# Hybrid decoder trunk: another order of the experts behind the first pair, and routing by token halves

## The chip, the cores and the metric

One Trainium2 chip, one of its cores. The time is device microseconds (us) of one execution of the whole program, taken as the median of several runs. The program has no collective and one launch.

## The reference, cut to what matters

Two layers over 256 tokens of 1024 channels, all in 32-bit floats. Each layer is a mixer (windowed attention beside a gated linear recurrence), a LayerNorm, a feed-forward part and a second LayerNorm. The feed-forward part of layer 0 is one dense SwiGLU. That of layer 1 is a mixture of eight experts with 3584 hidden channels each, and every token goes to its two best experts:

```python
logits = jnp.einsum('bsd,de->bse', x, router_w).astype(f32)
top_val, top_idx = lax.top_k(logits, TOP_K)
top_p = jax.nn.softmax(top_val, axis=-1)
comb = jnp.sum(top_p[..., None] * jax.nn.one_hot(top_idx, N_EXPERTS, dtype=f32), axis=-2)
y = jnp.zeros(x.shape, f32)
for e in range(N_EXPERTS):
    y = y + comb[..., e:e + 1] * _swiglu(x, w_gate[e], w_up[e], w_down[e]).astype(f32)
```

The 256 tokens make 512 assignments to eight experts, some 64 per expert. The weights of all eight experts are read.

## The kernel before, in words

**The stream of weights.** All weights come in units of 1 MB (`WeightStream`, L46), in the order in which they are multiplied, on the one DMA queue of SyncE (SP). A unit is loaded (L104) when a slot of on-chip memory for it is free. There are five slots from the start; in layer 1 scratch memory is added bit by bit, the last of it at L1008 to L1015 (two of the split buffers, four slots `wx0` to `wx3` under the scratch of the mixer, and `ax`), so that the experts begin with 15 slots (14 once `ax` is taken back in block 0 of place 1). A unit that needs an expert's number (every unit of experts other than expert 0) has SP load the number from `idi` first.

**Wide and narrow experts.** The experts are worked through in eight places 0 to 7. Place 0 is always expert 0. The others are ranked by their token counts, and `SEQ[s]` (L39) is the rank that place `s` takes, `CAP[s]` (L40) the tokens it has room for. With 128 it is wide: each weight unit is split into a high and a low half (`_hi` on ScalarE, L125, `_lo` on VectorE, L143), and TensorE multiplies three times in `fp32r` (hi by hi, lo by hi, hi by lo). The slot is free after `_lo`, some units ahead of TensorE. With 64 it is narrow: the unit is multiplied as it is, in two halves of the array's columns, and the slot is free after TensorE.

An expert has seven blocks of 512 hidden channels with six units each (two gate, two up, two down), 42 units in all. Places 0 and 1 are interleaved block by block (`blocks`, L264); this is called the pair. Places 2 to 7 follow one after the other. The loop at L1226 does gate, Silu, up, the product, and then the down projection of the block before. `start_expert` (L1093) gathers an expert's tokens by multiplying them with a one-hot matrix, `finish_expert` (L1171) adds its output to the residual.

**The stretch before the experts (L985 to L1201).** The order on each engine is the order in which this Python emits it. The two halves of 128 tokens, t = 0 and 1, come out of the mixer's output projection one after the other. For each, VectorE subtracts the mean (`center`), TensorE transposes the result for the router, and `normalise` multiplies on VectorE (L959) and adds on GpSimd (POOL, L961). `logits` are 16 small matmuls, `select` (L974) finds each token's top two on VectorE in six small instructions. The positions of the tokens within each expert come from one set of matmuls for both halves (L1035), `expert_one_hot(0)` makes the one-hot matrix, `route_ranks` (L1178) ranks the experts by count in 16 small instructions on VectorE and writes their numbers to `idi`, and `start_expert(0)` gathers. Matmuls without use (`keep_warm`, L421) fill waits of TensorE. In the first block `route_experts` (L1203) works out the weights of the tokens and the capacities on VectorE.

Of the kernel before, what the change touches and what calls it, by code (L numbers as in the profile page):

```python
# [16 lines left out]
P = 128  # L17
# [7 lines left out]
E = 8  # L25
# [13 lines left out]
SEQ = (None, 3, 0, 4, 1, 5, 2, 6)  # L39
CAP = (128, 64, 128, 64, 128, 64, 64, 64)  # L40
# [5 lines left out]
class WeightStream:  # L46
    def __init__(self, tc, pool, units):
        self.nc = tc.nc
        self.units = units
        self.loaded = 0  # L50
        self.n_hi = 0
        self.n_lo = 0
        self.taken = 0
        self.w = {}
        self.hl = {}
        self.owner = {}
        self.free = [(pool, f"w{j}") for j in range(NW_BASE)]
        self.ring = {p: [(pool, f"{p}{j}") for j in range(NHI)] for p in ("hi", "lo")}
        self.first = None
        self.after = {}  # L60
        self.lent = None

# [20 lines left out]
    def _fill(self):  # L83
        while self.free and self.loaded < len(self.units):
            self._load()

# [112 lines left out]
def trunk(ctx, tc, x, xT, w_in, w_out, prm, wbd, rb, ohc, cst, ln1_g, ln1_b, ln2_g, ln2_b,  # L199
# [115 lines left out]
    U = WeightStream(tc, wpool, units)  # L315

# [7 lines left out]
    jmask = csts[:, 256:384].rearrange("p (t a b) -> p t a b", t=2, a=8)  # L324
# [649 lines left out]
    def select(t, p):  # L974
        V.scalar_tensor_tensor(lg[:, t, :], p[:, 0:E], ln[t].mv[:, 1:2], rwb, op0=ALU.mult, op1=ALU.add)
        le = lg[:, t, :, None].to_broadcast([P, E, E])
        lj = lg[:, t, None, :].to_broadcast([P, E, E])
        c = cmp[:, t]
        V.tensor_tensor(out=c[:, :, 0, :], in0=lj, in1=le, op=ALU.is_equal)
        V.tensor_tensor(out=c[:, :, 0, :], in0=c[:, :, 0, :], in1=jmask[:, t], op=ALU.mult)  # L980
        V.tensor_tensor(out=c[:, :, 1, :], in0=lj, in1=le, op=ALU.is_gt)
        V.tensor_reduce(out=rank[:, t, :], in_=c.rearrange("p e a j -> p e (a j)"), op=ALU.add, axis=AX.X)
        V.tensor_scalar(sel[:, t, :], rank[:, t, :], 1.5, None, op0=ALU.is_lt)

# [15 lines left out]
    keep_warm(1, big())  # L1000
    for q in range(2):
        transpose_x(ax[:, 1, :], q, xf_emit(1))
    keep_warm(2, big())
    normalise(1)
    select(0, plg)
    select(1, logits(1))
    keep_warm(7, big())
# [10 lines left out]
    pos = rt.tile([P, 2, E], F32, name="pos")  # L1018
# [8 lines left out]
    cmp7 = ep.tile([P, E - 1, 2, E - 1], F32, name="cmp7")  # L1027
# [6 lines left out]
    pp = sm()  # L1034
    mm(pp[:, 0:2 * E], trir, sel.rearrange("p t e -> p (t e)"), True, False)  # L1035
    mm(pp[:, E:2 * E], onesr, sel[:, 0, :], False, True)
    pc = sm()
    for t in range(2):
        mm(pc[:, 0:E], onesr, sel[:, t, :], t == 0, t == 1)
    keep_warm(3, halves()[0])  # L1040
    V.tensor_copy(pos, pp[:, 0:2 * E].rearrange("p (t e) -> p t e", t=2))
# [51 lines left out]
    def start_expert(s):  # L1093
        wide = CAP[s] == P
        g = [ep.tile([P, KC, CAP[s]], F32R if wide else F32, name=f"g{s}_{i}", tag="g", bufs=3)
             for i in range(1 + wide)]

        def dst(a, p):
            A.activation(g[0][:, a, :], p, AF.Copy)
            if wide:  # L1100
                V.tensor_tensor(out=g[1][:, a, :], in0=p, in1=g[0][:, a, :].bitcast(F32), op=ALU.subtract)  # L1101

        gather(ohe[s], dst, CAP[s])
        st[s] = g
# [73 lines left out]
    def route_ranks():  # L1178
        V.tensor_copy(cnt8, pc[:, 0:E])
        n = E - 1  # L1180
        le = cnt8[:, 1:E, None].to_broadcast([P, n, n])
        lj = cnt8[:, None, 1:E].to_broadcast([P, n, n])
        V.tensor_tensor(out=cmp7[:, :, 0, :], in0=lj, in1=le, op=ALU.is_equal)
        V.tensor_tensor(out=cmp7[:, :, 0, :], in0=cmp7[:, :, 0, :], in1=jmask[:, 0, 1:E, 1:E], op=ALU.mult)
        V.tensor_tensor(out=cmp7[:, :, 1, :], in0=lj, in1=le, op=ALU.is_gt)
        V.tensor_reduce(out=rank7, in_=cmp7.rearrange("p e a j -> p e (a j)"), op=ALU.add, axis=AX.X)
        for s in range(1, E):
            V.tensor_scalar(perm[:, s - 1, :], rank7, float(SEQ[s]), None, op0=ALU.is_equal)
        V.tensor_scalar(id7, iota[:, 1:E], UNSEL, None, op0=ALU.add)
        V.tensor_tensor(out=tmp7, in0=perm, in1=id7[:, None, :].to_broadcast([P, n, n]), op=ALU.mult)  # L1190
        V.tensor_reduce(out=id7, in_=tmp7, op=ALU.add, axis=AX.X)
        V.tensor_copy(idi, id7[0:1, :])

    expert_one_hot(0)
    V.tensor_reduce(out=mxl, in_=lg, op=ALU.max, axis=AX.X, negate=True)
    route_ranks()
# [4 lines left out]
    start_expert(0)  # L1201

    def route_experts():  # L1203
        n = E - 1
        V.tensor_tensor(out=pr, in0=pr, in1=selv, op=ALU.mult)
# [20 lines left out]
    for i, (s, b) in enumerate(blocks):  # L1226
# [6 lines left out]
        if i == 0:  # L1233
            route_experts()
        if (s, b) == (1, 0):
            assert U.lent is None
            ax = mxp.tile([P, 2, D], F32, name="axm", tag="ax")
            for t in range(2):
                scaled(t)
# [119 lines left out]
def _layout(i):  # L1359
# [67 lines left out]
    cst[:, 256:384] = np.tile((np.arange(8)[None] < np.arange(8)[:, None]).reshape(1, 64), 2)  # L1427
# [21 lines left out]
```

## Time and profile before

| what | value |
|---|---|
| time, median of 3 runs | 1282.12 us (1280.95 to 1283.67) |
| the profiled execution, its own time | 1284.04 us |
| its span, first to last instruction | 1282.3 us |
| TensorE busy with matmuls | 1224.8 us, 96% |
| VectorE busy | 647.4 us, 50% |
| ScalarE busy | 518.1 us, 40% |
| moved by DMA | 428.99 MB, 335 GB/s over the span |

The span is what the trace shows from the first to the last instruction; the time of the execution has 1.7 us more around it. A busy TensorE is not one at its peak: a matmul counts as busy while it is in the pipe. The DMA rate by slices of the span says more here, since the experts' weights come at one rate for long stretches.

### The profile page before, as it was taken

Reading aid. Unit: us, or ns where it says so; the run is one execution under the profiler, and the core shown is the slowest. Engines: PE = TensorE matmul, PEld = TensorE weight load, DVE = VectorE, ACT = ScalarE, POOL = GpSimd, SP = SyncE. Lnnn points to the kernel's source line nnn. Section 1 sums busy time; section 2 is a strip of 40 time slices with the busy share of each in tenths; the row PEclk is TensorE's granted clock in tenths of the full one; section 3 lists DMA queues with packets and bytes.
Section 4 is the critical chain, followed back from the end, with each engine's and each line's share of the span. In section 5 each row is a group of like instructions: output and inputs, shape, how many; then the busy total and the mean of one; then the engine's idle time right before and its main releaser. Section 6 shows DMA issues by size and latency. Waiting matters only on the chain. (4 is left out here: it accounts for less than half of the span.)

```text
span 1282.3 us, 18541 instructions
## 1 busy us (share of the span) xinstructions
PE 1224.8 (96%) x7564; PEld 911.7 (71%) x7564; DVE 647.4 (50%) x616; ACT 518.1 (40%) x549; POOL 81.0 (6%) x75
## 2 busy tenths in 40 slices
PE   9999999999999899999999999999999999799884
PEld 8979999999987776666678875568886554354441
DVE  6597544457688753445588841069882001001004
ACT  5674443344683542444467731057762000000001
POOL 3124000004022010000000000000000000000001
PEclk9999999999999999999999999999999999999998
DMA  9843545554377769999999979999999999999994
GB/s 350 310 176 143 208 176 196 198 213 150 149 285 276 272 249 415 420 421 420 421 420 414 367 278 420 420 420 421 421 421 392 420 420 421 420 420 420 421 420 180
DMA packets 63506, 428.99 MB, mean 335 GB/s; under 512 B 7951, under 2 KB 8376, under 8 KB 12984
## 3 DMA queue, kind: packets, MB, share of 16 engines
q1 hardware_dynamic: 62408, 423.55, 81.8%
q0 software_dynamic: 720, 3.68, 0.8%
q8 instruction: 61, 1.00, 0.3%
q10 hardware_dynamic: 288, 0.52, 0.1%
q14 instruction: 29, 0.24, 0.0%
HBM read 426.67 MB, written 2.63 MB: 335 GB/s over the span
## 5 line engine op out<-in xcount | busy, mean ns | idle before, releaser
L143 DVE TENSOR_TENSOR lo<-w,hi 128x2048 fp32r<-128x2048 f32 (+1 forms) x181 | 402.6, 2242 | 88.5 <-ACT hi L125 87.4
L125 ACT ACTIVATE hi<-w 128x2048 fp32r<-128x2048 f32 (+1 forms) x183 | 340.6, 1875 | 92.3 <-PE sm L240 52.8
L240 PE MATMUL sm<-w,g 128*64 128x256 f32 x2240 | 265.8, 382 | 4.3 <-DMA w<-in_moe_w_up_dram 4.2
L240 PEld LDWEIGHTS sm<-w,g 128*64 128x64 f32 x2240 | 159.2, 137 | 100.2 <-issue 23.7
L240 PE MATMUL sm<-hi,g 128*128 128x512 f32 x672 | 220.8, 400 | 1.5 <-DVE g L1101 1.5
L1242 DVE TENSOR_TENSOR h<-h,sm 128x256 f32<-128x256 f32 (+1 forms) x56 | 29.0, 518 | 294.7 <-PE sm L240 290.3
L240 PE MATMUL acc<-w,ht 128*64 128x512 f32 x560 | 141.5, 603 | 20.3 <-DMA w<-in_moe_w_down_dram 19.7
L1140 ACT ACTIVATE ht<-sm 128x256 f32<-128x256 f32 (+1 forms) x56 | 25.6, 457 | 322.4 <-PE sm L1138 322.4
L240 PEld LDWEIGHTS sm<-hi,g 128*128 128x128 f32 x672 | 126.7, 189 | 33.4 <-DVE g L1101 2.0
L240 PE MATMUL sm<-lo,g 128*128 128x512 f32 x336 | 133.7, 398 | 3.3 <-DVE lo L143 3.3
L240 PE MATMUL sm<-xh,hi 128*128 128x256 f32 x528 | 132.5, 284 | 0.0
L240 PE MATMUL sm<-xl,hi 128*128 128x256 f32 x528 | 132.0, 283 | 0.0
L240 PEld LDWEIGHTS acc<-w,ht 128*64 128x64 f32 x560 | 40.8, 138 | 99.2 <-issue 70.3
L240 PE MATMUL acc<-hi,ht 128*128 128x512 f32 x336 | 109.8, 398 | 0.0
L240 PEld LDWEIGHTS sm<-xh,hi 128*128 128x128 f32 x528 | 99.6, 189 | 1.7 <-issue 1.3
L240 PEld LDWEIGHTS sm<-xl,hi 128*128 128x128 f32 x528 | 99.8, 189 | 0.4
L240 PE MATMUL sm<-xh,lo 128*128 128x256 f32 x528 | 84.8, 283 | 0.0
L240 PEld LDWEIGHTS sm<-lo,g 128*128 128x128 f32 x336 | 63.5, 189 | 18.4 <-DVE lo L143 4.3
L240 PEld LDWEIGHTS acc<-hi,ht 128*128 128x128 f32 x336 | 63.0, 187 | 17.3 <-issue 2.7
L240 PEld LDWEIGHTS sm<-xh,lo 128*128 128x128 f32 x528 | 72.3, 189 | 0.0
L240 PE MATMUL acc<-lo,ht 128*128 128x512 f32 x168 | 67.1, 400 | 5.1 <-DVE lo L143 5.1
L353 POOL TENSOR_TENSOR mv<-mv,mhalf 128x1 f32<-128x1 f32 x8 | 7.0, 877 | 815.4 <-DVE mv L352 815.4
(263 smaller groups left out, 1177.7 us busy)
## 6 DMA issues: line engine op xcount, KB each, us to landing
w<-in_moe_w_gate_dram SPq DMA_DIRECT2D x112, 1024.0 KB, 13.7
w<-in_moe_w_up_dram SPq DMA_DIRECT2D x112, 1024.0 KB, 14.3
w<-in_moe_w_down_dram SPq DMA_DIRECT2D x110, 1024.0 KB, 15.7
w<-in_w_in_dram SPq DMA_DIRECT2D x18, 1024.0 KB, 6.1
w<-in_ffn_w_gate_dram SPq DMA_DIRECT2D x11, 1024.0 KB, 4.8
w<-in_ffn_w_up_dram SPq DMA_DIRECT2D x11, 1024.0 KB, 5.7
w<-in_ffn_w_down_dram SPq DMA_DIRECT2D x11, 1024.0 KB, 6.1
w<-in_w_out_dram SPq DMA_DIRECT2D x8, 1024.0 KB, 4.8
```

Source lines behind the costliest of these rows:

```text
L125: self.nc.scalar.activation(hi[a], w[a], AF.Copy)
L143: V.tensor_tensor(out=lo[a], in0=w[a], in1=hi[a].bitcast(F32), op=ALU.subtract)
L240: T.matmul(o, l, r, start=first, stop=last)
L353: G.tensor_tensor(out=o, in0=o, in1=mhalf, op=ALU.pow)
L1140: A.activation(ht[0], p[:, 0:nj, :], AF.Copy)
L1242: V.tensor_tensor(out=h, in0=h, in1=pu, op=ALU.mult)
```

## The change

It has four parts. (1) `SEQ` and `CAP` change: behind the pair the places are narrow, wide, narrow, wide, narrow, narrow, in place of wide, narrow, wide, narrow, narrow, narrow. The ranks that get 128 and 64 places stay the same. (2) The router's work is done for each half of the tokens by itself: half 0 is selected before half 1 is normalised, and expert 0's gather is done in two parts (`first_gather`), for half 0 while half 1 is still being selected, accumulating in two banks that are held meanwhile. Its one-hot matrix `oh0` lies in slot 8 of the mixer's scratch; the one in the place of before is made in the first block instead, for `finish_expert` alone. Ten of the 13 matmuls without use go. (3) `route_ranks` compares one key per expert (eight times the count, less the expert's number) in place of counts with a rule for ties, and takes 7 instructions in place of 16; it stands behind the gather's evictions. (4) Loads stop at a limit, before the first unit that needs an expert's number, until `route_ranks` has been emitted (`open`).

```diff
-SEQ = (None, 3, 0, 4, 1, 5, 2, 6)
-CAP = (128, 64, 128, 64, 128, 64, 64, 64)
+SEQ = (None, 3, 4, 0, 5, 1, 2, 6)
+CAP = (128, 64, 64, 128, 64, 128, 64, 64)
...
     def _fill(self):
-        while self.free and self.loaded < len(self.units):
+        while self.free and self.loaded < self.limit:
             self._load()
+
+    def open(self):
+        self.limit = len(self.units)
+        self._fill()
...
+    U.limit = len(units) - len(blocks) * 6 + [s for s, _ in blocks].index(1) * 6 - 2
...
-    jmask = csts[:, 256:384].rearrange("p (t a b) -> p t a b", t=2, a=8)
+    jmask = csts[:, 256:320].rearrange("p (a b) -> p a b", a=8)
+    seqc = csts[:, 320:369].rearrange("p (a b) -> p a b", a=7)
+    koff = csts[:, 369:376]
+    ids7 = csts[:, 376:383]
...
+    pos = rt.tile([P, 2, E], F32, name="pos")
+    oh0 = mpool.tile([P, 2, 1, P], F32, name="oh0", tag="m4_8")
+
+    def position(t):
+        p = sm()
+        mm(p[:, 0:E], trir, sel[:, t, :], True, t == 0)
+        if t:
+            mm(p[:, 0:E], onesr, sel[:, 0, :], False, True)
+        return p
+
+    def first_one_hot(t, p):
+        V.tensor_copy(pos[:, t, :], p[:, 0:E])
+        V.tensor_scalar(oh0[:, t, 0, :], iota, pos[:, t, 0:1], None, op0=ALU.is_equal)
...
     plg = logits(0)
     keep_warm(1, big())
+    select(0, plg)
     for q in range(2):
         transpose_x(ax[:, 1, :], q, xf_emit(1))
+    normalise(1)
+    ppos = position(0)
+    plg = logits(1)
+    first_one_hot(0, ppos)
+    select(1, plg)
+    pgx = [sm(4), sm(4)]
+
+    def first_gather(t, ks):
+        for k in ks:
+            mm(pgx[k // 4][:, k % 4, :], xt[t][:, k * P:(k + 1) * P], oh0[:, t, 0, :], t == 0 and k % 4 == 0, t == 1 and k % 4 == 3)
+
+    first_gather(0, range(KC))
+    ppos = position(1)
     keep_warm(2, big())
-    normalise(1)
-    select(0, plg)
-    select(1, logits(1))
-    keep_warm(7, big())
+    first_one_hot(1, ppos)
+    first_gather(1, range(KC))
+    pc = sm()
+    for t in range(2):
+        mm(pc[:, 0:E], onesr, sel[:, t, :], t == 0, t == 1)
...
-    pp = sm()
-    mm(pp[:, 0:2 * E], trir, sel.rearrange("p t e -> p (t e)"), True, False)
-    mm(pp[:, E:2 * E], onesr, sel[:, 0, :], False, True)
-    pc = sm()
-    for t in range(2):
-        mm(pc[:, 0:E], onesr, sel[:, t, :], t == 0, t == 1)
-    keep_warm(3, halves()[0])
-    V.tensor_copy(pos, pp[:, 0:2 * E].rearrange("p (t e) -> p t e", t=2))
...
-        gather(ohe[s], dst, CAP[s])
+        if s == 0:
+            for q in range(2):
+                dst(slice(q * 4, q * 4 + 4), pgx[q])
+        else:
+            gather(ohe[s], dst, CAP[s])
...
     def route_ranks():
-        V.tensor_copy(cnt8, pc[:, 0:E])
         n = E - 1
+        V.scalar_tensor_tensor(cnt8[:, 1:E], pc[:, 1:E], float(E), koff, op0=ALU.mult, op1=ALU.add)
         le = cnt8[:, 1:E, None].to_broadcast([P, n, n])
         lj = cnt8[:, None, 1:E].to_broadcast([P, n, n])
-        V.tensor_tensor(out=cmp7[:, :, 0, :], in0=lj, in1=le, op=ALU.is_equal)
-        V.tensor_tensor(out=cmp7[:, :, 0, :], in0=cmp7[:, :, 0, :], in1=jmask[:, 0, 1:E, 1:E], op=ALU.mult)
-        V.tensor_tensor(out=cmp7[:, :, 1, :], in0=lj, in1=le, op=ALU.is_gt)
-        V.tensor_reduce(out=rank7, in_=cmp7.rearrange("p e a j -> p e (a j)"), op=ALU.add, axis=AX.X)
-        for s in range(1, E):
-            V.tensor_scalar(perm[:, s - 1, :], rank7, float(SEQ[s]), None, op0=ALU.is_equal)
-        V.tensor_scalar(id7, iota[:, 1:E], UNSEL, None, op0=ALU.add)
-        V.tensor_tensor(out=tmp7, in0=perm, in1=id7[:, None, :].to_broadcast([P, n, n]), op=ALU.mult)
+        V.tensor_tensor(out=cmp7, in0=lj, in1=le, op=ALU.is_gt)
+        V.tensor_reduce(out=rank7, in_=cmp7, op=ALU.add, axis=AX.X)
+        V.tensor_tensor(out=perm, in0=seqc, in1=rank7[:, None, :].to_broadcast([P, n, n]), op=ALU.is_equal)
+        V.tensor_tensor(out=tmp7, in0=perm, in1=ids7[:, None, :].to_broadcast([P, n, n]), op=ALU.mult)
         V.tensor_reduce(out=id7, in_=tmp7, op=ALU.add, axis=AX.X)
         V.tensor_copy(idi, id7[0:1, :])
 
-    expert_one_hot(0)
+    U.ahead(1)
+    start_expert(0)
+    route_ranks()
+    U.open()
     V.tensor_reduce(out=mxl, in_=lg, op=ALU.max, axis=AX.X, negate=True)
-    route_ranks()
     U.ahead(3)
     for t in range(2):
         A.activation(pr[:, t, :], lg[:, t, :], AF.Exp, bias=mxl[:, t:t + 1])
     A.activation(zs, mxl, AF.Silu)
-    start_expert(0)
...
         n = E - 1
+        V.tensor_copy(cnt8, pc[:, 0:E])
...
         if i == 0:
             route_experts()
+            expert_one_hot(0)
```

## Rows read from the trace of the kernel before

**Rows 1.** The page: DMA rate in 40 slices of 32.06 us.

```profile
GB/s 350 310 176 143 208 176 196 198 213 150 149 285 276 272 249 415 420 421 420 421 420 414 367 278 420 420 420 421 421 421 392 420 420 421 420 420 420 421 420 180
```

**Rows 2.** Stretches: length, busy us by engine, granted clock, DMA share, GB/s.

```profile
404.00:480.00 76.00, 69.48 (x361) 55.24 (x361) 53.02 (x85) 39.19 (x31) 8.23 (x4) 0.96 0.63 238
412.00:414.00 2.00, 2.00 (x12) 2.00 (x11) 1.94 (x3) 0.68 (x2) 0.00 (x0) 0.51 0.00 0
```

**Rows 3.** Single loads, places 2 (second unit), 3, 4, 5 (first), 6 (second).

```profile
L104 SPq DMA_DIRECT2D w<-in_moe_w_gate_dram x1: 333/333/333, 600.3 to 600.3; - x1
DMA to landing us min/median/max: 12.4/12.4/12.4
...
L104 SPq DMA_DIRECT2D w<-in_moe_w_gate_dram x1: 333/333/333, 711.6 to 711.6; - x1
DMA to landing us min/median/max: 4.8/4.8/4.8
...
L104 SPq DMA_DIRECT2D w<-in_moe_w_gate_dram x1: 333/333/333, 817.0 to 817.0; - x1
DMA to landing us min/median/max: 18.9/18.9/18.9
...
L104 SPq DMA_DIRECT2D w<-in_moe_w_gate_dram x1: 333/333/333, 923.6 to 923.6; - x1
DMA to landing us min/median/max: 16.8/16.8/16.8
...
L104 SPq DMA_DIRECT2D w<-in_moe_w_gate_dram x1: 333/333/333, 1030.9 to 1030.9; - x1
DMA to landing us min/median/max: 19.8/19.8/19.8
```

**Rows 4.** Timeline of TensorE: first matmuls of places 2 to 6.

```profile
631.57 0.40 PE L240 MATMUL sm<-hi,g 128*128 128x512 f32 x1
...
755.99 1.30 PE L240 MATMUL sm<-w,g 128*64 128x256 f32 x10
...
842.59 0.49 PE L240 MATMUL sm<-hi,g 128*128 128x512 f32 x1
843.88 0.50 PE L240 MATMUL sm<-lo,g 128*128 128x512 f32 x1 [0.81 <-DVE lo L143]
...
967.98 1.30 PE L240 MATMUL sm<-w,g 128*64 128x256 f32 x10
...
1054.39 1.90 PE L240 MATMUL sm<-w,g 128*64 128x256 f32 x16
```

**Rows 5.** Timeline before the experts: GpSimd's adds, VectorE's selection, TensorE's gather.

```profile
403.78 2.93 POOL L961 TENSOR_TENSOR xt<-xt,lnb 128x512 f32<-128x512 f32 x2 [0.93 <-DVE xt L959]
...
404.47 1.05 DVE L979 TENSOR_TENSOR cmp<-lg 128x64 f32<-128x64 f32 x1
...
407.61 0.23 DVE L979 TENSOR_TENSOR cmp<-lg 128x64 f32<-128x64 f32 x1
...
408.59 0.17 DVE L983 TENSOR_SCALAR sel<-rank 128x8 fp32r<-128x8 f32 x1
...
410.13 5.36 PE L240 MATMUL sm<-oh,xt 128*128 128x128 f32 x32
```

**Rows 6.** Timeline of VectorE, ranks to the fourth split, and TensorE's wait.

```profile
412.26 0.16 DVE L1192 CAST idi<-id 1x7 int32<-1x7 f32 x1
...
422.12 2.29 DVE L143 TENSOR_TENSOR lo<-w,hi 128x2048 fp32r<-128x2048 f32 x1 [4.08 <-ACT hi L125]
...
428.82 2.29 DVE L143 TENSOR_TENSOR lo<-w,hi 128x2048 fp32r<-128x2048 f32 x1
...
431.17 0.79 PE L240 MATMUL sm<-lo,g 128*128 128x512 f32 x1 [2.45 <-DVE lo L143]
```

**Rows 7.** Timeline of SP's queue: loads of units 12 and 13, 16 and 17.

```profile
390.03 1.05 SPq L104 DMA_DIRECT2D w<-in_moe_w_up_dram  x2
...
414.66 2.54 SPq L104 DMA_DIRECT2D w<-in_moe_w_gate_dram  x2
```

More of the change, by code (lines that the diff above doesn't have):

```diff
@@ L61, in __init__ @@
         self.lent = None
+        self.limit = None
     def add(self, slots):
@@ L979, in select @@
         V.tensor_tensor(out=c[:, :, 0, :], in0=lj, in1=le, op=ALU.is_equal)
-        V.tensor_tensor(out=c[:, :, 0, :], in0=c[:, :, 0, :], in1=jmask[:, t], op=ALU.mult)
+        V.tensor_tensor(out=c[:, :, 0, :], in0=c[:, :, 0, :], in1=jmask, op=ALU.mult)
         V.tensor_tensor(out=c[:, :, 1, :], in0=lj, in1=le, op=ALU.is_gt)
@@ L1017, in trunk @@
     pr = rt.tile([P, 2, E], F32, name="pr")
-    pos = rt.tile([P, 2, E], F32, name="pos")
     mxl = rt.tile([P, 2], F32, name="mxl")
@@ L1026, in trunk @@
     rank7 = ep.tile([P, E - 1], F32, name="rank7")
-    cmp7 = ep.tile([P, E - 1, 2, E - 1], F32, name="cmp7")
+    cmp7 = ep.tile([P, E - 1, E - 1], F32, name="cmp7")
     perm = ep.tile([P, E - 1, E - 1], F32, name="perm")
@@ L1426, in _layout @@
     cst[:, 384:512] = (n[:, None] < n[None]) - UNSEL * np.eye(P)
-    cst[:, 256:384] = np.tile((np.arange(8)[None] < np.arange(8)[:, None]).reshape(1, 64), 2)
+    cst[:, 256:320] = (np.arange(8)[None] < np.arange(8)[:, None]).reshape(1, 64)
+    cst[:, 320:369] = np.repeat(np.array(SEQ[1:], f), 7)
+    cst[:, 369:376] = -np.arange(1, 8)
+    cst[:, 376:383] = np.arange(1, 8)
     r["cst"] = cst
```

## The prediction

> **What bounds the kernel now.** I read the DMA rate over the span first, because the stream of weights is the longest thing in the program. From 481 us on it stands at 420 to 421 GB/s almost throughout, with two dips: slices 22 and 23 (705 to 769 us) at 367 and 278, and slice 31 (962 to 994 us) at 392 [rows 1]. The last slice holds the tail behind the last weights. So the end is set by the stream: when it gets going, 1 MB per 2.49 us (1.0486 MB at 421 GB/s), and what it loses on the way. TensorE's 96% is no bound by itself; what matters is where it holds slots so long that SP has nothing to issue.
>
> Before 480 us the stream is limited by slots: 404 to 480 us run at 238 GB/s, so (1 - 238/421) x 76 = 33 us pass without a load [rows 2]. There the loads follow TensorE's consumption, and a microsecond won on TensorE is a microsecond won by the stream.
>
> Single loads give the losses by place. Issue plus time to landing puts unit 2 of place 2 at 612.7 us, unit 1 of place 3 at 716.4, of place 4 at 835.9, of place 5 at 940.4, unit 2 of place 6 at 1050.7 [rows 3]. In between lie 41, 42, 42 and 43 units, at full rate 102.1, 104.6, 104.6 and 107.1 us. They took 103.7, 119.5, 104.5 and 110.3, so 1.6, 14.9, 0 and 3.2 us were lost, 19.7 together.
>
> The first matmuls of places 2 to 6 stand at 631.6, 756.0, 842.6, 968.0 and 1054.4 [rows 4]. A wide place takes TensorE 124.4 or 125.4 us, a narrow one 86.6 or 86.4, the stream 104.6 for either. So a wide place makes TensorE some 20 us later, a narrow one takes 18 us back. I call lateness the time from the landing of a place's first unit to its first matmul: 21.3 us at place 2 (631.6 less 610.3), 39.6 at place 3, 6.7 at 4, 27.6 at 5. The stream loses in the place behind a wide one: 14.9 us at a lateness of 39.6, 3.2 at 27.6. The difference, 11.7 for 12.0, says that lateness above some 24.5 us is lost one for one, as 14 slots of 2.49 us (35 us), less those in use, would have it.
>
> **The new order.** Pair, place 0 and 1, is as before, so TensorE reaches place 2 at the same lateness, 21.3 us or a little less (a narrow gather has half the columns), below 24.5. Place 2, now narrow, loses nothing to slots and would end at 21.3 + 86.5 - 104.6 = 3.2 us. That is less than is possible: at place 4 a wide expert began at 6.7 us and still waited 0.81 us for its first low half [rows 4]. So place 3 (wide) starts at about 6.7, as place 4 of before did, and ends at 6.7 + 20.9 = 27.6, which costs 3.2 us in place 4. That one ends at 27.6 + 86.4 - 107.8 = 6.2. Place 5 (wide) starts at 6.7 again, with its wider gather perhaps 0.7 later, and costs place 6 another 3.2 to 3.9 us. Places 6 and 7 are narrow; behind the last wide one two narrow ones take back 36 us, so TensorE waits for weights at the end as now. Losses after: 0 + 3.2 + 3.6, and the 1.6 of place 2, which no slot explains and which may stay or not. Saved: 19.7 - 8.4 = 11.3 us, or 12.9 without the 1.6. If the place behind each wide one loses 5 instead of 3.2 to 3.9, it is 8.1. I take 11.8.
>
> **The stretch before the experts.** It counts by when TensorE goes on in the second block, since the stream follows TensorE until 480 us. Before, that is at 431.17 us, where TensorE had waited 2.45 us for VectorE's fourth split, which starts at 428.82 and takes 2.29 [rows 6].
>
> Selection. Half 0's six instructions (about 1.4 us: the pace of 407.61 to the end of 408.59 [rows 5]) go ahead of half 1's normalisation, so GpSimd's two adds, which run from 403.78 for 2.93 us, end near 407.8 in place of 406.7. Under them the same comparison took 1.05 us and 0.23 us once they were over [rows 5]. In the new order half 0's one-hot matrix and half 1's comparison fall under them, so half 1 is selected at about 408.9, against 408.76 before. Nothing is won there.
>
> By the Trainium skill (SBUF — State Buffer, section "SBUF: two separate sides") VectorE and GpSimd share a pair of ports under a lock: a VectorE instruction with two inputs in SBUF, or in a mode that uses both ports, waits until GpSimd's whole instruction is over. The row with 1.05 against 0.23 us agrees for two inputs; for the one-hot instruction, with one input, the rows show nothing, and if it were free the sum would be up to 0.7 us better. This speaks against moving VectorE's work under the adds.
>
> Gather. It starts at about 410.0 as before (410.13), but with 16 instructions left of 32, which took 5.36 us [rows 5]. Part of that ran at a granted clock of 0.51, the lower of the two levels, 1.2 GHz [rows 2]. If half of the 32 ran so, one takes 0.112 us at full clock and 0.223 at half (mean 5.36/32 = 0.168), and 16 take 1.8 to 3.6 us. The gather ends at 411.8 to 413.6 instead of 415.5.
>
> VectorE then sets the pace. The last eviction of the gather is a copy and a subtraction of 512 columns; by a quarter of a split's 2.29 us for 2048 columns [rows 6] that is 0.6 us each, some 1.5 with the hand-over, so 413.3 to 415.1. Behind them stand `route_ranks` (7 instructions at some 0.25 us, 1.7), the maximum (0.2), splits 1 to 3 (3 x 2.29), `route_experts` (from the end of split 3 at 424.41 to 428.82, 4.4) with the added copy and two one-hot instructions (0.6, by 0.17 to 0.23 each [rows 5]), split 4 (2.3): 16.1 us, so 429.4 to 431.2 in place of 431.1. Before, VectorE had 4.08 us of idle time in this chain, waiting for ScalarE [rows 6]; that cover is used up. TensorE's wait ahead of split 4 grows by about what its gather gains and the split doesn't, 1 to 2 us, and if the clock then stands at its lower level as it did at 412 to 414 us [rows 2], that costs as much as it did the gather, 1.8 us (5.36 less twice 1.8). I take 0.6 us won, between 1.7 won and 1.5 lost. The ten matmuls without use that go stood in waits of TensorE and are worth nothing.
>
> SP. The experts' numbers (ready at 412.42 [rows 6]) come at about 415 to 417, behind the evictions. Loads 16 and 17, issued from 414.66 [rows 7], go out some 3 us later, and everything on SP's one queue behind them. They are needed behind the third wide block, at 467 us (431.2 and two blocks of 124.4/7 = 17.8 us), so this costs nothing while those 50 us stand. The larger delay is one the change doesn't name: `oh0` lies in slot 8 of the scratch, and by the sizes of the tiles that memory is the second extra weight slot. Unit 12, issued at 390.03 [rows 7], must now wait for the gather's last matmul, about 412 to 413, and units 13 to 15 and all later ones wait behind it on SP. It is needed in the up projection of the third block, which begins at 449; a third of a block on, that is 455. Five loads, 12.4 us, go into the 33 us in which the stream had nothing to do; I cost it at nothing.
>
> **The sum.** 11.8 + 0.6 = 12.4 us. From the profiled execution's own 1284.04 that is 1271.6; it stands 1.9 above the median of the runs, so by the median 1282.12 - 12.4 = 1269.7 us.
>
> **Rivals.** (a) The lateness isn't taken back as reckoned, because a narrow place is fed at the stream's pace once TensorE has caught up, or the limit lies lower than 24.5: both later switches lose 5 us more in sum, 1274.7. For it: the limit rests on two points. Against it: place 4 of before started from 6.7. Chance 0.10. (b) The loss belongs to the switch from wide to narrow whatever the lateness, and two switches lose as much as before: 14.9 once and 3.2, no gain but the 0.6, 1281.5. Against it: the second switch lost 3.2 only. 0.03. (c) The prologue gives more, if VectorE's chain is shorter than summed and TensorE keeps its full clock: up to 3.7 us (what the gather's end gains) in place of 0.6, 1266.6. Against it: the splits are VectorE's alone. 0.06. (d) Slower: unit 12 waits on SP so long that TensorE runs dry in the third block. Place: SP's load into the second extra slot. It costs TensorE one for one once the load goes out after 450 us (455 less 4.8 to land [rows 3]), and the whole is slower than before once it goes out after 462; at 465 it gives 1284.7. Against it: the gather it waits for ends near 413. 0.03.
>
> **How the numbers follow.** Forecast 0.78, rivals as above. 0.2% is 2.6 us, about what a measurement of this kernel can tell from no change. Faster: forecast, (a) and (c), 0.94 less 0.01 for a poor case of (a), 0.93. Within 0.2%: (b) and that, 0.04. Slower: (d), 0.03. The likeliest's own bounds are 8.1 - 1.5 and 12.9 + 1.7, 1275.5 and 1267.5. The range leaves out the last part of these and (b) and (d), and reaches to (c): 1266.5 to 1274.5.
>
> **What would show it.** In the rate by slices the dip of slices 22 and 23 is gone, and two dips like that of slice 31 stand behind places 3 and 5. Time from landing to first matmul of places 2 to 5 is about 21, 7, 27 and 7. The second block's split 4 ends at 429 to 431, TensorE idles 3 to 4 us before its end, loads of units 12 to 15 go out together near 413. The prediction is wrong if a dip of 10 us or more remains behind a wide place, if TensorE's first narrow matmul comes with the pair's lateness well above 24, or if TensorE goes on in the second block more than 2 us from 430.5.

## The result, and the profile after

The changed kernel took 1266.41 us (median of 4 runs, 1265.78 to 1267.72) against 1281.94 for the one before on the same chip: ratio 0.9879, 95% interval 0.9862 to 0.9896, 15.5 us faster (13.3 to 17.7). Forecast were 12.4, in a range from 1266.5 to 1274.5 us: the time lies 0.1 us below it. Span against span, the two profiled executions are 18.1 us apart (1264.2 and 1282.3), because that of before was 1.9 above its median and that of after 0.5 below.

The DMA rate of after in 40 slices of 31.6 us:

```profile
GB/s 349 311 193 144 203 178 200 200 200 151 167 247 186 367 266 396 421 420 420 420 420 419 420 421 420 421 415 422 420 420 420 420 421 402 421 420 420 420 421 169
```

The dips of before to 367 and 278 and to 392 [rows 1] are gone. What is left is 415 and 402, one slice each, where the places behind the wide ones begin (842 and 1054 us). They are 0.4 and 1.4 us of the full rate, and at the landings below nothing goes missing there beyond the regular gaps of the last section.

Lateness comes from two views: the timeline of TensorE at the first matmuls of places 2 to 6, and the single loads (place 2 second unit, places 3, 4, 5 first, place 6 second; issue, then time to landing).

```profile
628.84 0.44 PE L245 MATMUL sm<-w,g 128*64 128x256 f32 x2
...
715.53 0.51 PE L245 MATMUL sm<-hi,g 128*128 128x512 f32 x1
...
841.99 0.44 PE L245 MATMUL sm<-w,g 128*64 128x256 f32 x2
...
928.58 0.50 PE L245 MATMUL sm<-hi,g 128*128 128x512 f32 x1
...
1054.00 0.44 PE L245 MATMUL sm<-w,g 128*64 128x256 f32 x2
```

```profile
L109 SPq DMA_DIRECT2D w<-in_moe_w_gate_dram x1: 333/333/333, 597.6 to 597.6; - x1
DMA to landing us min/median/max: 12.5/12.5/12.5
...
L109 SPq DMA_DIRECT2D w<-in_moe_w_gate_dram x1: 333/333/333, 693.7 to 693.7; - x1
DMA to landing us min/median/max: 19.8/19.8/19.8
...
L109 SPq DMA_DIRECT2D w<-in_moe_w_gate_dram x1: 333/333/333, 798.4 to 798.4; - x1
DMA to landing us min/median/max: 19.7/19.7/19.7
...
L109 SPq DMA_DIRECT2D w<-in_moe_w_gate_dram x1: 332/332/332, 904.2 to 904.2; - x1
DMA to landing us min/median/max: 19.8/19.8/19.8
...
L109 SPq DMA_DIRECT2D w<-in_moe_w_gate_dram x1: 333/333/333, 1012.0 to 1012.0; - x1
DMA to landing us min/median/max: 20.3/20.3/20.3
```

Lateness is, as in the prediction, the time from the landing of a place's first unit to its first matmul. The landings are 610.1, 713.5, 818.1, 924.0 and 1032.3. Lateness at places 2 to 6 is therefore 21.2, 2.0, 23.9, 4.6 and 24.2 (a second unit lands 2.49 after the first). The four stretches between the landings took 103.4, 104.6, 105.9 and 108.3 us, against 102.1, 104.6, 104.6 and 107.1 at full rate. So 1.3, 0, 1.3 and 1.2 were lost, 3.8 in place of the 19.7 of before: 15.9 us saved.

The rest of the 18.1 us between the spans lies ahead of the experts. The timelines of before and after show the mixer's last addition, and in after the stretch behind it (VectorE, TensorE, GpSimd, SP, in the order of their starts, a few of many rows):

```profile
399.67 0.75 DVE L811 SCALAR_TENSOR_TENSOR ax<-sm,ra,ax 128x512 f32<-128x512 f32 x1 [0.33 <-PE sm L240]
```

```profile
397.53 0.75 DVE L820 SCALAR_TENSOR_TENSOR ax<-sm,ra,ax 128x512 f32<-128x512 f32 x1 [0.33 <-PE sm L245]
...
401.87 3.27 PE L245 MATMUL sm<-rwg,xf 128*128 128x8 f32 x16
...
402.42 2.90 POOL L970 TENSOR_TENSOR xt<-xt,lnb 128x512 f32<-128x512 f32 x2 [1.71 <-DVE xt L968]
...
403.05 1.11 DVE L1006 TENSOR_SCALAR oh<-csts,pos 128x128 f32<-128x128 f32 x1
...
404.99 3.76 PE L245 MATMUL sm<-oh,xt 128*128 128x128 f32 x16
...
406.41 0.17 DVE L992 TENSOR_SCALAR sel<-rank 128x8 fp32r<-128x8 f32 x1
...
408.40 0.35 PE L245 MATMUL sm<-sel,trir 128*128 128x8 f32 x1
...
409.21 0.29 DVE L1006 TENSOR_SCALAR oh<-csts,pos 128x128 f32<-128x128 f32 x1
...
409.64 2.02 PE L245 MATMUL sm<-oh,xt 128*128 128x128 f32 x16
...
411.70 0.80 SPq L109 DMA_DIRECT2D w<-in_moe_w_up_dram  x2
...
414.34 0.16 DVE L1221 CAST idi<-id 1x7 int32<-1x7 f32 x1
...
428.34 0.50 PE L245 MATMUL sm<-lo,g 128*128 128x512 f32 x1 [2.84 <-DVE lo L148]
```

The mixer ended 2.1 us sooner in this execution, in code that the change doesn't touch. The whole of it comes up at one place of the first layer (VectorE, before, then after):

```profile
61.16 0.69 DVE L668 TENSOR_TENSOR P<-sm,bias_t 128x512 f32<-128x512 f32 x1 [2.31 <-DMA bias_t<-vr]
```

```profile
58.89 0.68 DVE L677 TENSOR_TENSOR P<-sm,bias_t 128x512 f32<-128x512 f32 x1
```

In before VectorE waited 2.31 us there for a DMA of the attention's bias, in after it didn't. That part is scatter between executions, not the change, so all below is counted from the mixer's last addition. TensorE goes on with split 4 at 30.8 us behind it, against 31.5 before [rows 6]: 0.7 won, 0.6 forecast. 15.9 and 2.1 and 0.7 make 18.7, for the 18.1 that the spans show. Unrounded, and counted at the landings alone, it closes: 2.1 to the mixer's last addition, 0.5 from there to place 2's second unit (213.1 us before, 212.5 after), 15.7 up to place 6's second unit, less 0.3 by which the tail behind the last weights was longer.

### The profile page after: what moved, and what is told of

It is laid out like the page before. It is cut to its first block, busy times and chain, and to the rows that moved or that the text cites. A ratio compares the mean times of both kernels' runs of the same rounds, so it can differ in the third digit from the quotient of the medians.

```text
span 1264.2 us, 18520 instructions
## 1 busy us (share of the span) xinstructions
PE 1218.9 (96%) x7555; PEld 911.5 (72%) x7555; DVE 646.5 (51%) x611; ACT 518.3 (41%) x549; POOL 81.7 (6%) x75
## 5 line engine op out<-in xcount | busy, mean ns | idle before, releaser
L245 PE MATMUL sm<-w,g 128*64 128x256 f32 x2240 | 262.1, 382 | 2.6 <-DMA w<-in_moe_w_up_dram 2.5
L1173 ACT ACTIVATE ht<-sm 128x256 f32<-128x256 f32 (+1 forms) x56 | 25.6, 457 | 308.6 <-PE sm L1171 308.6
L245 PE MATMUL acc<-w,ht 128*64 128x512 f32 x560 | 136.1, 602 | 11.2 <-DMA w<-in_moe_w_down_dram 10.7
## 6 DMA issues: line engine op xcount, KB each, us to landing
w<-in_moe_w_gate_dram SPq DMA_DIRECT2D x112, 1024.0 KB, 17.8
```

The costliest lines, as they stand in the source:

```text
L245: T.matmul(o, l, r, start=first, stop=last)
L1173: A.activation(ht[0], p[:, 0:nj, :], AF.Copy)
```

## The experiments

Gains are by the ratio to the kernel before on the same chip, times 1282 us, with the 95% interval; the changed kernel's own stands at 15.5 (13.3 to 17.7).

**The order alone.** In the kernel before:

```diff
-SEQ = (None, 3, 0, 4, 1, 5, 2, 6)
-CAP = (128, 64, 128, 64, 128, 64, 64, 64)
+SEQ = (None, 3, 4, 0, 5, 1, 2, 6)
+CAP = (128, 64, 64, 128, 64, 128, 64, 64)
```

> The kernel before with the new order of places alone (SEQ and CAP of the change), nothing else. Theory (slots): of the gain of 15.5 us by the medians nearly all is the loss of the stream behind wide places, so this kernel wins 14.8 (15.5 less the 0.7 that the prologue showed against the mixer's last addition) and at most 15.8: about 1267 us, and no two neighbouring slices of the DMA rate below 415 GB/s from 506 us to the last slice. Rival (the prologue and what it does to the stream's start carry 3 us or more): 1269.5 us or above. Lateness at places 3 and 5 (first unit's landing to first matmul) 2 to 5 us and at places 4 and 6 about 24 in either case.

It took 1268.90 us against 1283.77, ratio 0.9885 (0.9867 to 0.9904), a gain of 14.7 us (12.3 to 17.1). Place 3 started at a lateness of 2.0, place 5 at 6.1; places 4 and 6 at 25.6 and 25.5. The slices of its page from 506 us on read 419 to 421 but for 409 and 395, which lie alone, so the order alone has nearly all of the gain. The rival with 3 us in the prologue is left only at the edge of the interval, and the landings of the next run speak against it.

**Everything but the order.** The changed kernel with the two lines of before put back.

> The changed kernel with the old order of places (64, 128 alternating: SEQ and CAP of before), so the routing, the first gather and the key ranks of the change alone. Theory: 0.7 us faster than before, 1281.2 us, between 1280 and 1282; the second block goes on about 30.8 us behind the mixer's last addition, against 31.5 before; the dips of the DMA rate at 705 to 769 us and near 980 us are back. Rival (the prologue is worth 3 us or more): 1279 us or less, with the same 30.8 us or fewer.

1281.69 us against 1283.77, ratio 0.9986 (0.9975 to 0.9997): 1.8 us (0.4 to 3.2). The second block goes on 30.6 us behind the mixer's last addition, and the dips in the rate are back (366 and 284, and 388). The mechanism is as expected and the size is between theory and rival. The difference goes with TensorE's clock behind its wait for split 4: windows of after, and of the kernel of the run with `oh0` moved, told below, which has the same prologue (this run's own window, 428 to 432 us, reads 1.00 too).

```profile
429.00:433.00 4.00, 4.00 (x15) 3.12 (x13) 4.00 (x3) 0.51 (x1) 0.00 (x0) 0.57 1.01 420
```

```profile
428.00:432.00 4.00, 4.00 (x19) 3.06 (x20) 4.00 (x3) 1.13 (x1) 0.00 (x0) 1.00 0.76 262
```

The granted clock fell to its lower level, 1.2 GHz, behind a wait of 2.84 us in the one, and not behind one of 2.87 in the other. It fell in the executions profiled of before, of the order alone, of after and of the next two runs, not in this one. Unit 40 of the experts (counted from 0, as in the prediction), where the stream has reached full rate, lands 105.9 us behind the mixer's last addition before and 106.1 with the order alone; with the new prologue 105.3 and 105.4 where the clock fell, 103.8 in the two where it didn't. So the prologue wins 0.6 us, and 2.1 when the clock stays up. In both profiles of the old prologue the clock fell, so how much of the other 1.5 us belongs to the prologue and how much to chance is not shown.

**Two wide places in a row.** The changed kernel with:

```diff
-SEQ = (None, 3, 4, 0, 5, 1, 2, 6)
-CAP = (128, 64, 64, 128, 64, 128, 64, 64)
+SEQ = (None, 3, 4, 5, 0, 1, 2, 6)
+CAP = (128, 64, 64, 64, 128, 128, 64, 64)
```

> The changed kernel with its two later wide places next to each other: places 2 to 7 take 64, 64, 128, 128, 64, 64 tokens. Theory (what lateness exceeds about 24.5 us is lost one for one): lateness 21 at place 2, some 3 at place 3 and some 2 at place 4 (TensorE waits for weights there), 22 to 24 at place 5 and 42 to 44 less the loss behind it, so the stream loses 18 to 20 us during place 5, lateness stands near 24.5 at place 6, and the time is 1266.4 + 19 = 1285.4 us, 1283 to 1288. Rival (a price of each switch from a wide to a narrow place, 15 at the most as before behind place 2): one switch less, 1281.5 us at most. Rival (two narrow places in a row cost TensorE its lead as well): 1290 us or more.

1284.36 us against 1283.77, ratio 1.0008 (0.9996 to 1.0020): the gain of 15.5 is gone, and 1.0 us more (0.5 faster to 2.6 slower). Lateness at places 2 to 5 was 21.2, 1.5, 2.7 and 23.2. The rate by slices, the second unit of place 6 and TensorE's first matmul there:

```profile
GB/s 351 314 188 144 206 173 181 195 229 157 143 293 156 396 244 421 421 421 419 420 420 420 419 421 419 421 421 420 421 419 388 359 361 303 421 420 419 421 420 171
```

```profile
L109 SPq DMA_DIRECT2D w<-in_moe_w_gate_dram x1: 333/333/333, 1032.5 to 1032.5; - x1
DMA to landing us min/median/max: 8.1/8.1/8.1
...
1074.57 0.65 PE L245 MATMUL sm<-w,g 128*64 128x256 f32 x4
```

Four slices, 388, 359, 361 and 303, hold the loss: it begins within the second wide place, as lateness passes the limit, and not at the switch. From place 5's first landing to place 6's second unit 115.6 us passed in place of 107.1, 8.5 lost (1.3 in the change). Lateness there is 36.5 (1074.6 less 1038.1), and from there to the last units 13.1 more were lost (1.3 in the change). In sum that is 19 us more than in the change, as expected; but the expectation had all of it lost within place 5 and a lateness near 24.5 at place 6. A price per switch would have made this kernel no slower than before, and the time alone hardly tells that apart; the place and the size of the dips do.

**One slot less.** The changed kernel with:

```diff
-NW_EXTRA = 4
+NW_EXTRA = 3
```

> The changed kernel with three extra weight slots in place of four. Theory (the limit of lateness is set by the slots, 2.49 us each): the stream is behind TensorE by one unit less from the start, 2.5 us lost ahead of place 2, the limit is 22.0, and lateness of 23.9 and 24.3 at places 4 and 6 loses 1.9 and 2.3: 6.7 us in sum, 1273.1 us, 1271 to 1275; the DMA rate shows small dips behind places 3 and 5. Rival (the slots set the start alone, and what was lost behind wide places has another cause): 1268.9 us and no dips. Rival (slots are no limit): 1266.4 us.

1272.43 us against 1283.77, ratio 0.9905 (0.9886 to 0.9924), a gain of 12.2 us (9.7 to 14.6): 3.3 less than with all slots, for 6.7 expected. Unit 40 lands 2.7 us later behind the mixer's last addition, as expected (2.5). Behind the wide places, at lateness 24.0 and 24.2, the stream lost only 1.9 us more than after did, for 4.2 expected. So a slot is worth 2.49 us at the start. A limit of 24.5 less 2.49 doesn't give the 1.9; the corrected limit of the next section, some 25.8, does. Time alone doesn't exclude the first rival.

**The loads that wait for the gather.** The changed kernel with `oh0` in memory that no weight slot covers:

```diff
-    oh0 = mpool.tile([P, 2, 1, P], F32, name="oh0", tag="m4_8")
+    oh0 = mpool.tile([P, 2, 1, P], F32, name="oh0", tag="m4_1")
```

> The changed kernel with the first expert's one-hot matrix in scratch slot 1, memory that no extra weight slot covers, in place of slot 8. Theory (unit 12's wait for the gather falls into time in which the stream has nothing else to do): units 12 to 15 are issued near 390 us instead of 412, the second block goes on at the same 30.8 us behind the mixer's last addition, and the time is the same within 0.5 us, 1266.4. Rival (the late loads cost the stream or crowd those of the next units): 1.5 to 3 us less, 1264.

1266.13 us, ratio 0.9879 (0.9863 to 0.9896), the same as the change. SP's queue:

```profile
387.53 0.96 SPq L109 DMA_DIRECT2D w<-in_moe_w_up_dram  x2
388.54 14.71 SPq L109 DMA_DIRECT2D w<-in_moe_w_down_dram  x2
416.56 2.52 SPq L109 DMA_DIRECT2D w<-in_moe_w_gate_dram  x2
```

Unit 12 goes 24 us sooner than in the change (387.53 for 411.70) and unit 40 lands at 103.8 behind the mixer's last addition, as in the run with the old order and the late load, which had 103.8 too. The wait that looked largest on SP costs nothing.

**The clock behind TensorE's wait of 0.71 us.** The changed kernel with three matmuls without use in it:

```diff
+    keep_warm(3, big())
     normalise(1)
     ppos = position(0)
```

> The changed kernel with three matmuls of 512 columns without use in TensorE's wait of 0.71 us ahead of the first half's positions. Question: is it that wait that brings the granted clock to 0.5 for 6.8 us behind it? If so: logits of half 1 take 2.0 us in place of 3.27 and the first half's gather 1.8 in place of 3.76, half 1 is selected 1.2 us sooner, the second block goes on 1.2 to 2 us sooner (28.8 to 29.6 us behind the mixer's last addition), 1264.5 to 1265.2 us. If the clock falls anyway (the many short matmuls ahead of it): 30.8 to 31.0 and 1266.4.

1265.98 us, ratio 0.9879 (0.9863 to 0.9896). TensorE:

```profile
401.41 0.94 PE L245 MATMUL big<-onesr 128*128 128x512 f32 x3
402.36 0.24 PE L245 MATMUL sm<-sel,trir 128*128 128x8 f32 x1
402.47 1.93 PE L245 MATMUL sm<-rwg,xf 128*128 128x8 f32 x16
404.89 2.72 PE L245 MATMUL sm<-oh,xt 128*128 128x128 f32 x16 [0.49 <-DVE lg L984]
```

The logits took 1.93 us in place of 3.27 and the first half's gather 2.72 in place of 3.76, but half 1's selection now ran into GpSimd's second addition, where one comparison took 1.06 us in place of 0.23, so half 1 was selected only 0.3 us sooner. The second block goes on at 29.6, 1.3 us sooner than in the change, as expected. In the time that is too little to be seen. In the run with the three parts of `route_experts`, below, the logits took 1.93 us without these matmuls, so the wait alone doesn't bring the clock down each time.

**The gather split.** The changed kernel with:

```diff
-    first_gather(0, range(KC))
+    first_gather(0, range(4))
     ppos = position(1)
-    keep_warm(2, big())
+    first_gather(0, range(4, KC))
```

> The changed kernel with the positions of token half 1 between the eighth and the ninth matmul of the first half's gather, without the two fillers that stood behind them. Theory (VectorE's chain from the evictions on sets when the second block goes on, and it hangs on the gather's end): in the changed kernel half 1 was selected at 406.58 but its positions came behind all 16 matmuls, at 408.40; they come some 1.5 us sooner, the gather's second half 0.75 us sooner, and the second block goes on 30.1 us behind the mixer's last addition in place of 30.8; time 0.7 us less, 1265.7. Rival (the chain behind is bound by something else): 30.8 and no change.

1267.69 us, ratio 0.9898 (0.9881 to 0.9915), 13.1 us (10.9 to 15.3): nothing won. The positions come at 406.25, but the 24 gather matmuls behind them took 4.53 us, and the second block goes on at 30.6. Windows of this kernel:

```profile
405.00:409.00 4.00, 3.90 (x19) 3.64 (x19) 1.46 (x7) 0.14 (x1) 0.10 (x1) 0.50 0.02 4
...
416.00:420.00 4.00, 3.64 (x10) 2.86 (x11) 4.00 (x3) 1.94 (x2) 0.00 (x0) 0.61 1.01 428
```

The granted clock stayed low through the gather, and fell once more behind the wait for split 1.

**The old ranking in the new order of work.** The changed kernel with the comparisons of before in `route_ranks`:

```diff
...
-        V.tensor_tensor(out=cmp7, in0=lj, in1=le, op=ALU.is_gt)
-        V.tensor_reduce(out=rank7, in_=cmp7, op=ALU.add, axis=AX.X)
-        V.tensor_tensor(out=perm, in0=seqc, in1=rank7[:, None, :].to_broadcast([P, n, n]), op=ALU.is_equal)
+        V.tensor_tensor(out=cmp7[:, :, 0, :], in0=lj, in1=le, op=ALU.is_equal)
+        V.tensor_tensor(out=cmp7[:, :, 0, :], in0=cmp7[:, :, 0, :], in1=jmask[:, 1:E, 1:E], op=ALU.mult)
+        V.tensor_tensor(out=cmp7[:, :, 1, :], in0=lj, in1=le, op=ALU.is_gt)
+        V.tensor_reduce(out=rank7, in_=cmp7.rearrange("p e a j -> p e (a j)"), op=ALU.add, axis=AX.X)
+        for s in range(1, E):
+            V.tensor_scalar(perm[:, s - 1, :], rank7, float(SEQ[s]), None, op0=ALU.is_equal)
...
```

> The changed kernel with the old way of ranking the experts (two comparisons and a mask for ties, seven single comparisons with the order's numbers), all else as changed. Theory (in the new order VectorE has no idle time between the first evictions and split 4, so each instruction there counts): 8 instructions more at about 0.17 to 0.25 us, 1.6 us, put split 4 and the second block 1.6 us later, 32.4 us behind the mixer's last addition in place of 30.6 to 30.9, and the time up by 1 to 1.6 us, 1267.4 to 1268. Rival (there is still room, as in the kernel before, where VectorE waited 4.08 us for ScalarE in this stretch): 30.8 and 1266.4.

1267.59 us, ratio 0.9878 (0.9857 to 0.9898): no difference that can be told. The ranks take 2.3 us in place of 1.5, where 1.6 more were expected, since the seven single comparisons take 0.60 us together:

```profile
414.50 0.60 DVE L1221 TENSOR_SCALAR perm<-rank 128x7 f32<-128x7 f32 x7
```

The second block goes on 31.4 behind the mixer's last addition, 0.6 later than in the change. So VectorE's chain does set it, and with the old ranks the second block goes on where it did before (31.5): the key ranks carry what the prologue won there.

**`route_experts` later, in three parts.** The changed kernel with the positions in the second block, the weights in the third, the counts and the one-hot matrix in the fourth (`route_experts` is cut into the three functions named here):

```diff
...
         if i == 0:
-            route_experts()
+            V.tensor_copy(cnt8, pc[:, 0:E])
+        elif i == 1:
+            route_positions(pos, posq)
+        elif i == 2:
+            route_weights()
+        elif i == 3:
+            route_counts()
             expert_one_hot(0)
```

> The changed kernel with route_experts cut into three: the positions in the second block, the weights in the third, the counts and expert 0's one-hot matrix in the fourth (narrow, without splits). Theory (before 480 us the stream follows TensorE one for one): TensorE's wait of 2.84 us ahead of split 4 goes, with it the lower clock behind it (3.4 us at half rate, 1.7 us), nothing of the same size comes back in blocks 2 to 4, and the time falls by 2.5 to 4.5 us, to 1262 to 1264. Rival (VectorE has no room there, the wait is only moved): 1266.4, with a wait of 2 us or more in the second or third block. Rival (the stream doesn't follow TensorE): the wait goes and the time stays at 1266.4.

1262.53 us, ratio 0.9854 (0.9838 to 0.9871), a gain of 18.7 us (16.5 to 20.8), 3.2 more than the change. The two intervals overlap, but the four times (1260.4 to 1264.0) lie below all four of the kernel with `oh0` moved on the same chip (1265.3 to 1267.0). The wait for split 4 is gone from TensorE's timeline, only that for split 1 (1.75 us) is left, and the windows from 409 to 436 us show the full clock throughout. Unit 40 lands at 99.7 in place of 105.3 behind the mixer's last addition. The profiled execution is the fastest of the four, and 1.0 of these 5.6 us came ahead of split 1 (18.3 us behind the addition, for 19.3), where half 1's logits ran at the full clock, which is not the edit's doing. Further on, lateness at places 2 to 6 is as in the change (21.3, 2.0, 24.0, 4.5, 24.0). The stream follows TensorE before 480 us, as the prediction had it.

**All of it together.** The ranks go ahead of the first gather's evictions, the maximum and the exponentials behind half 1's selection, counts and positions between the halves of the gather, beside the three parts of `route_experts`:

```diff
...
     U.ahead(1)
-    start_expert(0)
     route_ranks()
     U.open()
-    V.tensor_reduce(out=mxl, in_=lg, op=ALU.max, axis=AX.X, negate=True)
+    start_expert(0)
     U.ahead(3)
...
```

> The kernel with route_experts in three parts (e6), and in addition half 1's positions and the counts between the two halves of the first gather, the maximum and the exponentials right behind half 1's selection, and the key ranks ahead of the first gather's evictions, in VectorE's idle time there. Theory (VectorE's chain from the gather to the first three splits sets TensorE's first wait of 1.75 us): 1.5 us of VectorE's work leaves the chain, the wait of 1.75 us ahead of the second weight unit falls below 0.6, and the time is 1 to 2 us below that of e6: 1260.5 to 1261.5. Rival (what the chain gains the lower clock takes back, as where the gather alone was split): 1262.5, with TensorE at a granted clock below 0.8 somewhere between 411 and 425 us.

1262.70 us, ratio 0.9837 (0.9813 to 0.9861), 20.9 us (17.8 to 24.0). TensorE's wait for split 1 fell from 1.75 to 0.22 us, as expected. But the granted clock was 0.50 to 0.57 from 405 to 416 us, and unit 40 landed at 100.5, no sooner than without these moves, as the rival had it. The times don't decide: the gain is 2.2 us above that of the three parts alone, and the intervals overlap. With the three matmuls without use added:

> e8 with three matmuls of 512 columns without use in TensorE's wait ahead of the first half's positions. Theory: logits of half 1 and a part of the first gather at full clock, which brought the second block forward by 1.2 us against the mixer's last addition when done alone: 0.5 to 1.2 us below e8, about 1260. Rival (VectorE's chain doesn't hang on the gather any more): the same as e8.

1260.20 us, ratio 0.9824 (0.9804 to 0.9844), 22.6 us (20.0 to 25.1): the fastest median here, below both kernels of the study. Unit 40 lands at 100.4 again, so the last step is not shown to come from where it was expected. With the three parts and the three matmuls only:

> e6 with the three matmuls without use alone. Theory: VectorE's chain hangs on the end of the first gather, which comes about 0.6 us sooner (11.05 us behind the mixer's last addition in place of e6's, on the same clock): 0.5 to 1.2 us below e6, about 1261.7. Rival: no change, 1262.5.

1262.87 us, ratio 0.9836 (0.9816 to 0.9857), 21.0 us (18.3 to 23.6). The medians show no change against the three parts alone, the ratios 2.3 us more, which can't be told from none. In the trace the split that TensorE waits for first came 1.2 us sooner (17.1 us behind the mixer's last addition, for 18.3), as the theory had it, but behind that wait of 1.76 us the clock fell to 0.50 for some 3 us, and unit 40 landed at 100.2. The three last runs' intervals overlap with each other and with that of the three parts alone.

## Where the prediction held, and where it failed

**The step that failed** is the floor under lateness: "That is less than is possible", with place 3 starting at about 6.7 and place 4 losing 3.2, place 5 starting at 6.7 again and place 6 losing 3.6. This term of the losses, 6.8 us, measured nothing: the 1.3 and 1.2 us that these two stretches lost are regular gaps at the landings, told in the last section. The arithmetic that the prediction had set aside was right: 21.2 + 86.7 (628.84 to 715.53) less the 105.9 from landing to landing is 2.0, the lateness measured. From 2.0 and 4.6 a wide place reaches 23.9 and 24.2, below the limit, and nothing is lost. The 6.7 of before's place 4 was no floor. It was what the loss behind place 2 had left: 39.6 less 15 lost, less the 18 that a narrow place takes back. The wait of 0.81 us for a low half [rows 4], read as a sign of the floor, is only how a wide place begins. The second matmuls of places 3 and 5 in after:

```profile
717.86 0.50 PE L245 MATMUL sm<-lo,g 128*128 128x512 f32 x1 [1.82 <-DVE lo L148]
...
929.88 0.50 PE L245 MATMUL sm<-lo,g 128*128 128x512 f32 x1 [0.80 <-DVE lo L148]
```

Place 3 began at a lateness of 2.0 with a wait of 1.82 us, and place 5 at 4.6 with one of 0.80, as long as that at 6.7 in before.

**The limit was there, 1.3 us higher.** Lateness above a limit is lost one for one, as the prediction had it. But its two points hold one of the regular gaps each, 1.3 us at the experts' units 144 and 219 of before; those units had been issued 8 and 15 us before they landed, against 4.8 where the stream had run dry [rows 3], so no slot was missing. Without the gaps a lateness of 39.6 lost 13.6 us and one of 27.6 lost 1.9, and the limit is 26.0 or 25.7 in place of 24.5. With two wide places in a row 113.9 us passed from place 6's second unit to place 7's first (1040.6 to 1154.5) in place of 102.1: 11.8 lost, 1.2 of it in a gap, so 10.6 at a lateness of 36.5, which gives 25.9. At 23.9, 24.0 and 24.2 nothing was lost beyond the gaps. In the seven profiled executions where places 4 and 6 stood at 25.5 to 25.7 about 1 us more was lost up to the end. With one slot less a limit of 25.8 becomes 23.3, and lateness of 24.0 and 24.2 should lose 0.7 and 0.9, 1.6 together; 1.9 were measured. The 1.6 of place 2, "which no slot explains", was such a gap too, and it stayed.

**What stayed.** The prediction took the 3.2 behind place 4 of before as slots alone. The stretch held one of those gaps; 3.8 us of gaps stay in after, and no loss by slots. So 19.7 less 3.8 is 15.9, in place of 11.8: 4.1 more than forecast.

**Prologue.** Forecast 0.6 won, measured 0.7 behind the same point, by nearly the steps forecast: with 2.1 us added to after's times for the mixer's earlier end, half 1 is selected at 408.7 (forecast 408.9), the first expert's gather ends at 413.8 (411.8 to 413.6), the evictions at 415.2 (413.3 to 415.1), and TensorE goes on at 430.5 (429.4 to 431.2), behind a wait of 2.84 us (3 to 4). That half 1 came on time is luck: its logits ran at the lower clock (3.27 us, where 1.93 were measured at the full one), so its comparison fell behind GpSimd's additions and took 0.23 us, where the forecast had it under them with 1.05. Gather and evictions lie at the late end because all of the first half's gather, 3.76 us, ran at the lower clock. The forecast named the price if the clock stands low behind the wait for split 4, 1.8 us; the executions differ by 1.5 there. The one-hot matrix, left open in the prediction, took 1.11 us under GpSimd's additions and 0.29 behind them; it ended at 404.16, which is 0.29 us behind the first of the two additions (402.42 and half of 2.90), so the 0.7 us that a free one would have won was rightly left out. The Trainium skill (SBUF — State Buffer, section "SBUF: two separate sides") has a VectorE instruction in a mode that uses both ports wait until GpSimd's whole instruction is over. The trace agrees if the instruction ran in such a mode, which no row shows.

**SP.** Unit 12 was loaded at 413.8 by the same count (forecast 412 to 413), the numbers came at 416.6 (415 to 417), at no cost, as forecast and as the run with `oh0` moved shows. Rivals (a), (b) and (d) fall: behind the two switches the landings lost the gaps alone, and TensorE didn't run dry. Of (c) a part is true: 1266.4 is its time, but the order brings it, and the prologue only 0.6 to 2.1.

By the traces the sum is 15.9 + 0.7 = 16.6, and 18.0 where the clock stays up; measured by the medians are 15.5 (13.3 to 17.7), 14.7 for the order alone and 1.8 for the rest. The traces' sums lie in the upper part of the interval or 0.3 above it.

## What to carry to other kernels

Where a stream through a few slots is the bound, keep an account of lateness by stage: add what a stage costs the engine over the stream, take off what it gives back, and compare the peak with what the slots hold (take regular gaps out of the points that this limit is read from); then order the stages so that the peak stays below it. Don't put a floor under such an account because a row shows a small wait: ask first which part of the account that row already is. Once the loss is gone, the time follows whatever starts the stream, and there a few microseconds of small instructions on one engine, moved to where it is idle, were worth more (3.2 us) than the rest of what was rearranged ahead of the experts (1.8).

## What the runs showed of the hardware that had not been expected

- TensorE's clock falls behind waits of the same length in some executions and not in others. Behind a wait of 2.84 and of 2.87 us, at the same place of the code, it was 0.57 in one and 1.00 in the other. At the start of place 3, where TensorE waits for the first low half for some 2 us, the stretch from 714 to 730 us had a mean granted clock of 0.89 in the run with `oh0` moved and of 1.00 in after; place 3 took 128.0 and 126.5 us, and the 1.5 us is the difference between a lateness of 25.5 and 23.9 at place 4.

```profile
714.00:730.00 16.00, 14.17 (x55) 10.43 (x57) 9.72 (x6) 9.14 (x7) 0.00 (x0) 0.89 1.01 420
```

```profile
713.00:730.00 17.00, 15.08 (x66) 10.03 (x64) 9.96 (x6) 9.97 (x7) 0.00 (x0) 1.00 1.01 420
```

- In every kernel the landings of the full stream have a gap of mostly 1.2 to 1.7 us about every 70 units: in after around the experts' units 35, 104, 178, 250 and 312, where 1.2 to 1.4 us more passed between landings than the units take. Slots were free there: from unit 104 on the loads had been issued 16 to 21 us before they landed. In after each gap falls together with a packet of the instruction queue (q8, 16 KB, 1 us and more on one of the 16 DMA engines: 6.3% of them in the first row), and it is every eighth such packet: the second row counts those from the gap at unit 104 up to the one at 178. The packets between leave no mark at the landings, and the rate of the whole stream doesn't fall at unit 104 (420 GB/s in that slice, where 1.2 us without data would leave 404). One engine that falls behind while the others run ahead would look like that; no run tried it.

```profile
q8 instruction: 1, 0.02, 6.3%
...
q8 instruction: 8, 0.13, 0.3%
```
